# An encoder layer on one core: where softmax's 1/sum and the second sequence's 1/rms are multiplied in

## The chip, the cores and the metric

The kernel runs on one core of a Trainium2 chip. The metric is the device time of one execution in microseconds (us). The core has five engines that run their own instruction queues in order and wait for one another by semaphores: TensorE (PE in the profile; its weight loads are PEld), VectorE (DVE), ScalarE (ACT), GpSimd (POOL) and SyncE (SP), which here issues most of the DMAs. Matmul results land in PSUM, which has eight banks of 128 x 512 fp32 values; everything else is in SBUF or, for data that doesn't fit, in DRAM.

## The reference

One encoder layer is applied to two sequences of 512 tokens (`x_prompt`, sequence 0, and `x_sample`, sequence 1; 1024 channels each) with the same weights, all in fp32:

```python
x = x + 0.5 * swiglu(rms_norm(x, ffn1_norm), ...)
h = rms_norm(x, mix_norm)
proj = h @ w_in            # attention q, k, v; mLSTM q, k, v, gates; output gate; two merge gates
...
s = einsum('bqkgd,bskd->bkgqs', q, k) * scale     # 8 heads of 64, 2 k/v heads
p = softmax(s, axis=-1)
att = einsum('bkgqs,bskd->bqkgd', p, v)
mem = mlstm_bidirectional(...)                    # 4 heads of 128, sigmoid(o_pre) gate
merged = sigmoid(g_att) * (att @ w_up_att) + sigmoid(g_mlstm) * (mem @ w_up_mlstm)
x = x + merged @ w_out
x = x + 0.5 * swiglu(rms_norm(x, ffn2_norm), ...)
```

Two places of it matter here. Softmax divides the exponentials of each row by their sum; the division can as well be done after the product with v. And `rms_norm` multiplies each token's row by 1/rms, a number per token; since `h @ w_in` is linear, that factor can be applied to the row before the projection or to the projection's result.

## The kernel before

**Precision.** PE multiplies in a fast fp32 form that keeps fewer bits, so every operand is kept as a pair, high half and low half: `split` writes high = src rounded by an ACT copy, low = src - high by a DVE subtraction. A product is three matmuls (high x high, high x low, low x high). Channels (or heads) lie on the 128 partitions and the 512 tokens along the columns, except in the token-major projections for k, v and q, where tokens lie on the partitions.

**Order of the stages.** The first FFN serves both sequences together, then `mix(0)` and `mix(1)` do attention, mLSTM, merge and output projection of one sequence each, partly interleaved, and then the second FFN. `mix` is a generator; its callers step it. In the profiled execution the attention of sequence 0 lies at 714 to 824 us, that of sequence 1 at 1106 to 1210 us.

**What decides who runs when.** The program is written as a list of instructions with a priority that follows the program's order; `shifted(n)` gives the instructions inside it a later (or earlier) place by n. A scheduler makes each engine's queue from priorities, dependences, its own costs and free buffers. Buffers come from tagged rings: `t2` has 11 row buffers of 128 x 512, `f2` has 4, the small tiles have a ring each. PSUM has rings too: `MM` 3 banks, `PO` 1, `PS` 2, `PT` 2.

**Units and fill.** A projection by 128 columns of `w_in` is a unit: load (or fetch from DRAM, if sequence 0 has split and parked it) a weight, 24 matmuls into an `MM` bank, and a `done` function that empties the bank. `queue` holds the units for the merge gate of attention (`att_gate`) and the output gate (`out_gate`); `fill(n)` emits n of them between the heads of attention, so that PE has them to work on beside attention's own short chains.

**Where 1/rms is applied.** The rows that enter the projections are x * gain (`emit_hl`, L143), without 1/rms. `r[s]` is 1/rms with tokens on partitions, `R[s]` the same repeated over all partitions with tokens along the columns. Every `done` function multiplies: by `r[s]` as the scale of an ACT copy where tokens lie on partitions (`kv_done`, `q_done`, `mem_values`), by `R[s]` in a DVE multiplication where they lie along the columns (`mem_qk` L918, `out_gate` L927, `att_gate` L1045, `mem_gate` L1091). For sequence 1, `prep1` (L1335) makes the rows' two halves while sequence 0's `merge_mem` runs (after each of its 8 steps): it reads 128 channels of x back from `xbuf` by DMA and calls `emit_hl`.

**Attention.** For each head h, `scores(h)` does for each of four blocks of 128 queries: two matmuls into a `PS` bank (L1001), the negated row maximum on DVE (L1004), the exponential on ACT with the row sum as a second output (L1006), the reciprocal of the sum (L1007) and the scaling of the 128 x 512 exponentials by it in place (L1008), both on DVE. `attend(h)` turns the exponentials, four 128 x 128 transposes into a `PT` bank (L1020) for each of four blocks of keys, splits each bank (L657, L658) and accumulates with v in the one `PO` bank (L1028). The two halves of that bank are added (L1036, L1037) into 64 partitions of `af`; when the odd head of a pair is done, `af` (128 x 512, both heads) is split into `att`. The scores of head h + 1 are emitted ahead of `attend(h)`.

Of the kernel before, what the change touches and what calls it, by code (L numbers as in the profile page):

```python
# [8 lines left out]
F32 = mybir.dt.float32  # L9
F32R = mybir.dt.float32r  # L10
I32 = mybir.dt.int32
AF = mybir.ActivationFunctionType
# [4 lines left out]
P = 128  # L17
# [9 lines left out]
def encoder(ctx, tc, I, outs):  # L27
# [14 lines left out]
    def nm(s):  # L42
        n_id[0] += 1
        return f"{s}_{n_id[0]}"
# [15 lines left out]
    def T2(dtype=F32, tag="t2"):  # L60
        if tag in ("eb", "ac"):
            i = boxes[tag]
            boxes[tag] += 1
            return boxes["tile"][:, i % 4 + (4 if tag == "ac" else 0), :]
        if tag == "R":
            return spool.tile([P, S], dtype, tag="R", bufs=2, name=nm("R"))
        n = {"t2": 11, "f2": 4}[tag]
        return tpool.tile([P, S], dtype, tag=tag, bufs=n, name=nm(tag))
# [50 lines left out]
    def f(ap):  # L119
        return ap.bitcast(F32)  # L120
# [22 lines left out]
    def emit_hl(src, g, k, xh, xl):  # L143
        i1 = nc.scalar.activation(xh[:, k, :], src, AF.Copy, scale=g[:, k:k + 1])
        i2 = nc.vector.scalar_tensor_tensor(xl[:, k, :], src, g[:, k:k + 1], f(xh[:, k, :]),
                                       op0=ALU.mult, op1=ALU.subtract)
        return i1, i2
# [507 lines left out]
    def split(src, hi, lo, eng=None):  # L655

        nc.scalar.activation(hi, src, AF.Copy)  # L657
        (eng or V_).tensor_tensor(lo, src, f(hi), op=ALU.subtract)  # L658
# [4 lines left out]
    NEG = -1e30  # L663

    def small(w, tag):
        return spool.tile([P, w], F32, tag=tag, bufs=2 if tag != "asm" else 6, name=nm(tag))

    gm, g2 = [cpool.tile([P, KD], F32, name=nm("gain")) for _ in range(2)]
    gbias = cpool.tile([P, 16], F32, name="gbias")
# [86 lines left out]
        return p  # L756

    OUT = 3

    def mix(s, xh, xl, early=None, extra=None, after=None):  # L760

# [6 lines left out]

        def F2(dtype=F32):
            return T2(dtype, "f2")  # L770

        def win_cols(c0, done):
            return proj(win_v[:, :, c0:c0 + P], ("in", c0), xsrc, KD, done)
# [38 lines left out]

        def kv_done(pk):
            for b in range(4):
                nc.scalar.activation(kraw3[:, b, :], pk[b][:, 0:P], AF.Copy, scale=r[s][:, b:b + 1])
                nc.scalar.activation(Gt[:, b * 16:(b + 1) * 16], pk[b][:, 2 * P:2 * P + 16], AF.Copy,
                                     scale=r[s][:, b:b + 1])
                pv = pk[b][:, P:2 * P].rearrange("p (k e) -> p k e", k=HK)
                nc.scalar.activation(Vst[:, b, :, 0:DA], pv, AF.Copy, scale=r[s][:, b:b + 1])
                V_.scalar_tensor_tensor(Vst[:, b, :, DA:2 * DA], pv, r[s][:, b:b + 1], f(Vst[:, b, :, 0:DA]),  # L820
                                        op0=ALU.mult, op1=ALU.subtract)
            ssk = small(8, "ssk")
            sumsq(kraw, ssk)
            ko = rope_apply(kraw, rstd_cols(ssk, 8, DA), tabs[1], None)
            ko3 = ko.rearrange("p (g e) -> p g e", e=DA)
            nc.scalar.activation(kst[:, :, 0, 0, :], ko3, AF.Copy)
            nc.scalar.activation(kst[:, :, 0, 1, :], ko3, AF.Copy)
            V_.tensor_tensor(kst[:, :, 1, 0, :], ko3, f(kst[:, :, 0, 0, :]), op=ALU.subtract)
            V_.tensor_tensor(kst[:, :, 1, 1, :], ko3, f(kst[:, :, 0, 1, :]), op=ALU.subtract)
# [3 lines left out]
        def q_done(pq):  # L833
            ssq = small(32, "ssq")
            for b in range(4):
                t = T2()
                nc.scalar.activation(t, pq[b], AF.Copy, scale=r[s][:, b:b + 1])
                sumsq(t, ssq[:, b * 8:(b + 1) * 8])
                qraw.append(t)
            rq.append(rstd_cols(ssq, 32, DA))  # L840
# [56 lines left out]
        def mem_values():  # L897
            def done(pvv):
                vm = A([P, 2, 4, S], F32R, "Vm")
                for b in range(4):  # L900
                    nc.scalar.activation(vm[:, 0, b, :], pvv[b], AF.Copy, scale=r[s][:, b:b + 1])
                    V_.scalar_tensor_tensor(vm[:, 1, b, :], pvv[b], r[s][:, b:b + 1], f(vm[:, 0, b, :]),
                                            op0=ALU.mult, op1=ALU.subtract)
                Vm.append(vm)
            return tok_proj(xh, xl, [(1792, 512)], 2, done)

# [2 lines left out]
        def mem_qk(h, j):  # L909
            def done(pp):  # L910
                if j == 0 and not s:
                    t = wpool.tile([P, 4, S], F32R, tag="w8", bufs=4, name=nm("qk"))
                    qks[h] = [t[:, i] for i in range(4)]
                elif s:
                    t = wpool.tile([P, 2, S], F32R, tag="wr", bufs=4, name=nm("qk"))
                    qks.setdefault(h, []).extend(t[:, i] for i in range(2))
                t = F2()
                V_.tensor_tensor(t, pp, R[s], op=ALU.mult)  # L918
                split(t, *qks[h][2 * j:2 * j + 2])
            return win_cols((768, 1280)[j] + h * P, done)  # L920

        ogs = {}
# [1 line left out]
        def out_gate(h):  # L924
            def done(pp):
                og = T2(F32, "ac")
                V_.tensor_tensor(og, pp, R[s], op=ALU.mult)  # L927
                nc.scalar.activation(og, og, AF.Tanh, scale=0.5)
                G_.tensor_scalar(og, og, 1.0, hn[:, h:h + 1], op0=ALU.add, op1=ALU.mult)
                ogs[h] = og  # L930
            return win_cols(2320 + h * P, done)
# [60 lines left out]
        att = A([P, 4, 2, S], F32R, "att")  # L992
        afs = {}

        def scores(h):
            hk = h // 4
            Ps = []
            for b in range(4):
                p = PS()
                for j in range(2):  # L1000
                    nc.tensor.matmul(p, qT[:, h, b * P:(b + 1) * P], kv[:, hk * 2 + j, :],  # L1001
                                     start=(j == 0), stop=(j == 1))
                c = small(3, "asm")
                V_.tensor_reduce(c[:, 0:1], p, axis=AX.X, op=ALU.max, negate=True)  # L1004
                e = T2()
                nc.scalar.activation(e, p, AF.Exp, bias=c[:, 0:1], accum_out=c[:, 1:2])  # L1006
                V_.reciprocal(c[:, 2:3], c[:, 1:2])  # L1007
                V_.tensor_scalar(e, e, c[:, 2:3], None, op0=ALU.mult)  # L1008
                Ps.append(e)
            return Ps  # L1010

        def attend(h, Ps):
            hk = h // 4
            po = PO()
            turned = []
            for kb in range(4 + 1):
                if kb < 4:
                    p = PT()
                    for b in range(4):
                        nc.tensor.transpose(p[:, b * P:(b + 1) * P], Ps[b][:, kb * P:(kb + 1) * P], ident)  # L1020
                    ph, pl = T2(F32R), T2(F32R)
                    split(p, ph, pl)
                    turned.append((kb, ph, pl))
                if kb >= 1:
                    kv_, *pp = turned.pop(0)
                    with shifted(50):
                        for i, w in enumerate(pp):
                            nc.tensor.matmul(po, Vst[:, kv_, hk, :], w, start=(kv_ == 0 and i == 0),  # L1028
                                             stop=(kv_ == 3 and i == 1))
            if h % 2 == 0:  # L1030
                afs[0] = T2(F32, "f2")
            af = afs[0]
            o0 = (h % 2) * DA
            o1 = DA - o0
            t = T2(F32, "f2")
            nc.scalar.activation(t[o0:o0 + DA, :], po[o1:o1 + DA, :], AF.Copy)  # L1036
            V_.tensor_tensor(af[o0:o0 + DA, :], po[o0:o0 + DA, :], t[o0:o0 + DA, :], op=ALU.add)  # L1037
            if h % 2:
                split(af, att[:, h // 2, 0, :], att[:, h // 2, 1, :])

        mg = A([P, KD, S], F32, "mg")

        def att_gate(d):
            def done(pp):
                V_.tensor_tensor(mg[:, d, :], pp, R[s], op=ALU.mult)  # L1045
                nc.scalar.activation(mg[:, d, :], mg[:, d, :], AF.Tanh, scale=0.5)
            return win_cols(2832 + d * P, done)

        queue.extend(att_gate(d) for d in range(KD))
# [38 lines left out]
        def mem_gate(d):  # L1088
            def done(pp):
                t = ths[d] = T2()  # L1090
                V_.tensor_tensor(t, pp, R[s], op=ALU.mult)  # L1091
                nc.scalar.activation(t, t, AF.Tanh, scale=0.5)
            return win_cols(3856 + d * P, done)

        def merge_mem(d):
# [239 lines left out]
    def prep1(d):  # L1335
        if d == 0:
            nhl[1] = xhl_tiles()
        xt = T2(F32, "f2")
        nc.sync.dma_start(xt, xbuf[1][:, d, :])
        emit_hl(xt, gm, d, *nhl[1])  # L1340

    ffn_down(I["ffn1_w_down"][0], rbuf[0], up.ring, tail, xbuf, done1, 7, mix_consts)

# [178 lines left out]
```

## Time and profile before

| | us |
|---|---|
| median of 3 runs | 2084.76 |
| lowest, highest | 2084.72, 2087.68 |
| the profiled execution's own time | 2083.45 |
| its span, first to last instruction | 2081.4 |
| PE busy | 2060.3 |
| DVE busy | 1573.6 |
| ACT busy | 895.4 |

The span is what the profile's views divide up; the profiled execution's time is 2.05 us longer than it. In the views a row of a group names line, engine, operation, result and operands, shapes and count, then the busy time of all in us and the mean of one in ns, then how long the engine stood idle before them and what ended that. A row by stage gives a stretch of the span, its length, and for each engine the busy time and the number of instructions in it. In a row of waits the engine and line that waited stand left of the arrow, who ended the wait right of it. Matmuls are pipelined: the recorded length of one reaches into the next, so start times tell their pace.

### The profile page before, as it was taken

The page shows a single profiled execution, that of the slowest core. Times are in us where ns is not written, and L with a number is a line of the kernel's source. Part 1 is how long each engine was busy: PE and PEld are TensorE (multiplying, and loading weights), DVE is VectorE, ACT ScalarE, POOL GpSimd, SP SyncE. Part 2 cuts the span into 40 slices and gives each one's busy share as a digit, 9 for nine tenths or more (in the row PEclk, how much of TensorE's full clock was granted, in tenths as well). Part 3 has the DMA queues.
Part 4 walks back from the last instruction along what each step waited for, and adds up shares of the span by engine and source line. Part 5 has one row for each costly group of instructions (what it writes and reads, how often), then busy time and mean ns, then how long its engine had stood idle before and what let it go on. Part 6 is the DMA issues. An engine that isn't in the chain of part 4 may idle for free.

```text
span 2081.4 us, 27314 instructions
## 1 busy us (share of the span) xinstructions
PE 2060.3 (99%) x9488; PEld 1694.0 (81%) x9488; DVE 1573.6 (76%) x2870; ACT 895.4 (43%) x1645; POOL 111.2 (5%) x122
## 2 busy tenths in 40 slices
PE   8999999999999999999999999999999999999998
PEld 6888888888888877888887788888888888888887
DVE  7888888786797899575568846555788888785797
ACT  6544444443234566463344543324444444442222
POOL 1000000001003012100120000002000000000010
PEclk9999999999999999999999999999999999999999
DMA  8656555699766655777685345677656555599753
GB/s 277 208 171 195 193 171 182 201 346 359 260 223 243 216 167 198 257 240 272 214 283 193 112 153 188 208 258 244 200 177 201 193 172 182 187 339 350 273 189 117
DMA packets 303161, 458.52 MB, mean 220 GB/s; under 512 B 20304, under 2 KB 170848, under 8 KB 302000
## 3 DMA queue, kind: packets, MB, share of 16 engines
q1 hardware_dynamic: 301152, 451.32, 64.4%
q0 software_dynamic: 1872, 5.46, 0.8%
q8 instruction: 75, 1.23, 0.2%
q14 instruction: 62, 0.51, 0.1%
HBM read 289.82 MB, written 166.89 MB: 219 GB/s over the span
## 4 chain that ended last, share of the span: by engine, by line
PE 92%; DVE 3%; DMA 3%; ACT 1%; issue 1%; SPq 0%; POOL 0%; DVEq 0%; ACTq 0%; POOLq 0%
PE mm L755 19%; PE pss L333 17%; PE pst L333 11%; PE mm L333 10%; PE mm L589 9%; PE pst L589 4%; PE pss L589 4%; PE mm L739 4%; PE pso L589 3%; PE pso L739 1%; PE pso L1028 1%; PE pso L1167 1%; PE pst L755 1%; PE pss L755 1%; PE pss L1117 1%; PE pst L1020 1%
## 5 line engine op out<-in xcount | busy, mean ns | idle before, releaser
L755 PE MATMUL mm<-xh,w 128*128 128x512 f32 x896 | 290.6, 394 | 0.0
L333 PE MATMUL pss<-xc,w 128*128 128x512 f32 x1056 | 256.4, 392 | 0.2 <-DVE t L364 0.2
L333 PE MATMUL mm<-xc,w 128*128 128x512 f32 x1056 | 253.5, 391 | 2.2 <-ACT w L291 1.4
L333 PE MATMUL pst<-xc,w 128*128 128x512 f32 x1056 | 253.8, 390 | 0.1
L333 PEld LDWEIGHTS pss<-xc,w 128*128 128x128 f32 x1056 | 197.0, 188 | 47.4 <-DVE t L364 6.7
L333 PEld LDWEIGHTS mm<-xc,w 128*128 128x128 f32 x1056 | 197.4, 188 | 45.2 <-ACT w L291 2.3
L333 PEld LDWEIGHTS pst<-xc,w 128*128 128x128 f32 x1056 | 198.2, 188 | 41.6 <-ACT t L368 0.5
L755 PEld LDWEIGHTS mm<-xh,w 128*128 128x128 f32 x896 | 167.4, 188 | 33.6
L589 PE MATMUL mm<-rt,w 128*128 128x512 f32 (+1 forms) x819 | 188.4, 385 | 0.0
L755 PE MATMUL mm<-xl,w 128*128 128x512 f32 x448 | 176.0, 393 | 0.0
L589 PEld LDWEIGHTS mm<-rt,w 128*128 128x128 f32 x819 | 151.4, 188 | 29.8
L291 ACT ACTIVATE w<-t 128x512 fp32r<-128x512 f32 x176 | 106.9, 627 | 138.6 <-issue 55.2
L292 DVE TENSOR_TENSOR w<-t,w 128x512 fp32r<-128x512 f32 x176 | 118.3, 689 | 55.1 <-ACT w L291 53.1
L333 PE MATMUL pss<-xc,f 128*128 128x512 f32 x528 | 126.9, 389 | 0.0
L333 PEld LDWEIGHTS pss<-xc,f 128*128 128x128 f32 x528 | 99.1, 188 | 20.6
L657 ACT ACTIVATE w<-wr 128x512 fp32r<-128x512 f32 x72 | 45.1, 632 | 138.6 <-PE pso L589 70.8
L657 ACT ACTIVATE w<-t 128x512 fp32r<-128x512 f32 x82 | 51.8, 632 | 107.6 <-PE pst L589 62.4
L755 PEld LDWEIGHTS mm<-xl,w 128*128 128x128 f32 x448 | 84.3, 188 | 16.7
L589 PE MATMUL pst<-rt,w 128*128 128x512 f32 x396 | 93.7, 389 | 0.0
L589 PE MATMUL pss<-rt,w 128*128 128x512 f32 x396 | 93.7, 389 | 0.0
L589 PEld LDWEIGHTS pst<-rt,w 128*128 128x128 f32 x396 | 74.3, 188 | 15.4
L589 PEld LDWEIGHTS pss<-rt,w 128*128 128x128 f32 x396 | 74.3, 188 | 15.4
(337 smaller groups left out, 3666.9 us busy)
## 6 DMA issues: line engine op xcount, KB each, us to landing
rt<-rbuf SPq DMA_DIRECT2D x154, 512.0 KB, 5.5
wpark<-w SPq DMA_DIRECT2D x104, 512.0 KB, 3.6
w<-wpark SPq DMA_DIRECT2D x104, 512.0 KB, 4.8
wr<-in_ffn_w_gate_dram SPq DMA_DIRECT2D x62, 512.0 KB, 5.3
rbuf<-tab SPq DMA_DIRECT2D x102, 256.0 KB, 3.8
wr<-in_ffn_w_up_dram SPq DMA_DIRECT2D x44, 512.0 KB, 4.7
rbuf<-f SPq DMA_DIRECT2D x72, 256.0 KB, 3.7
wr<-in_w_in_dram SPq DMA_DIRECT2D x36, 512.0 KB, 5.7
```

What stands on the lines that cost most here:

```text
L291: pin(nc.scalar.activation(t[:, 0], src, AF.Copy))
L292: pin(V_.tensor_tensor(t[:, 1], src, f(t[:, 0]), op=ALU.subtract))
L333: nc.tensor.matmul(p, a[:, k, :], xt[:, b, k, :], start=(first and k == 0 and i == 0), stop=(k == HK_ - 1 and i == 2), skip_group_check=True)
L589: nc.tensor.matmul(p, u[:, a, d * P:(d + 1) * P], r[:, b, ts], start=(first and q == 0 and k == 0), stop=(q == len(us) - 1 and k == 2), sk ...
L657: nc.scalar.activation(hi, src, AF.Copy)
L739: nc.tensor.matmul(p[b][:, :N], a[:, k, bs], w_[:, kl, :], start=(k == 0 and i == 0), stop=(k == KD - 1 and i == 2))
L755: nc.tensor.matmul(p, a[:, k, :], b, start=(k == 0 and i == 0), stop=(k == n - 1 and i == 2))
L1020: nc.tensor.transpose(p[:, b * P:(b + 1) * P], Ps[b][:, kb * P:(kb + 1) * P], ident)
L1028: nc.tensor.matmul(po, Vst[:, kv_, hk, :], w, start=(kv_ == 0 and i == 0), stop=(kv_ == 3 and i == 1))
L1117: nc.tensor.matmul(p, qk[a][:, isl], qk[b], start=(n == 0), stop=(n == 2))
L1167: nc.tensor.matmul(po, vm[:, a, t, hs_], b, start=(t == 0 and n == 0), stop=(t == 3 and n == 2))
```

## The change

Softmax's division is moved. The exponentials go into the transposes as they are. The row sums of a pair of heads are collected in one small tile `asum` (128 queries x 4 blocks x 2 heads). When the odd head of the pair has been added into `af`, DVE takes the reciprocal of the 8 columns, ACT writes them out repeated 64 times each into a 128 x 512 buffer (`wide`), PE turns that with four transposes into a `PT` bank (so that each of the pair's 128 partitions has its head's 1/sum along the tokens), DVE multiplies `af` by the bank, and `af` is split as before. All that follows the reciprocal is shifted by 30 places in priority. The ring of the maxima gets 4 buffers of one column instead of 6 of three.

For sequence 1 alone (`NORMED = (1,)`), the rows are multiplied by gain and 1/rms in one DVE instruction (`normed`, which the kernel has for the second FFN) and then split, ACT copy and DVE subtraction, where before ACT scaled the high half by the gain and DVE made the low half in one scalar_tensor_tensor. After the projections of sequence 1 nothing is multiplied by 1/rms any more: the ACT copies have scale 1, the q/k units of the mLSTM split straight from the PSUM bank, and the tanh of the gates reads the bank. Sequence 0 keeps its multiplications.

```diff
-        return spool.tile([P, w], F32, tag=tag, bufs=2 if tag != "asm" else 6, name=nm(tag))
+        return spool.tile([P, w], F32, tag=tag, bufs=2 if tag != "asm" else 4, name=nm(tag))
...
+    NORMED = (1,)
...
+        def col_scale(b):
+            return 1.0 if s in NORMED else r[s][:, b:b + 1]
+
+        def split_cols(src, b, hi, lo):
+            if s in NORMED:
+                return split(src, hi, lo)
+            nc.scalar.activation(hi, src, AF.Copy, scale=r[s][:, b:b + 1])
+            V_.scalar_tensor_tensor(lo, src, r[s][:, b:b + 1], f(hi), op0=ALU.mult, op1=ALU.subtract)
+
+        def scaled_row(pp, to):
+            if s in NORMED:
+                return pp
+            t = to()
+            V_.tensor_tensor(t, pp, R[s], op=ALU.mult)
+            return t
...
             def done(pp):       # mem_qk
-                t = F2()
-                V_.tensor_tensor(t, pp, R[s], op=ALU.mult)
-                split(t, *qks[h][2 * j:2 * j + 2])
+                split(scaled_row(pp, F2), *qks[h][2 * j:2 * j + 2])
...
             def done(pp):       # att_gate; out_gate and mem_gate likewise
-                V_.tensor_tensor(mg[:, d, :], pp, R[s], op=ALU.mult)
-                nc.scalar.activation(mg[:, d, :], mg[:, d, :], AF.Tanh, scale=0.5)
+                nc.scalar.activation(mg[:, d, :], scaled_row(pp, lambda: mg[:, d, :]), AF.Tanh, scale=0.5)
...
         def scores(h):
             hk = h // 4
             Ps = []
+            if h % 2 == 0:
+                asums[h // 2] = small(8, "asum").rearrange("p (b u) -> p b u", u=2)
...
-                c = small(3, "asm")
-                V_.tensor_reduce(c[:, 0:1], p, axis=AX.X, op=ALU.max, negate=True)
+                c = small(1, "asm")
+                V_.tensor_reduce(c, p, axis=AX.X, op=ALU.max, negate=True)
                 e = T2()
-                nc.scalar.activation(e, p, AF.Exp, bias=c[:, 0:1], accum_out=c[:, 1:2])
-                V_.reciprocal(c[:, 2:3], c[:, 1:2])
-                V_.tensor_scalar(e, e, c[:, 2:3], None, op0=ALU.mult)
+                nc.scalar.activation(e, p, AF.Exp, bias=c, accum_out=asums[h // 2][:, b, h % 2:h % 2 + 1])
...
             if h % 2:           # attend
-                split(af, att[:, h // 2, 0, :], att[:, h // 2, 1, :])
+                inv = asums[h // 2]
+                V_.reciprocal(inv, inv)
+                with shifted(30):
+                    wide = T2(F32, "f2")
+                    nc.scalar.activation(wide.rearrange("p (b u e) -> p b u e", u=2, e=DA),
+                                         inv.unsqueeze(3).to_broadcast([P, 4, 2, DA]), AF.Copy)
+                    pr = PT()
+                    for b in range(4):
+                        nc.tensor.transpose(pr[:, b * P:(b + 1) * P], wide[:, b * P:(b + 1) * P], ident)
+                    V_.tensor_tensor(af, af, pr, op=ALU.mult)
+                    split(af, att[:, h // 2, 0, :], att[:, h // 2, 1, :])
...
             nhl[1] = xhl_tiles()       # prep1
         xt = T2(F32, "f2")
         nc.sync.dma_start(xt, xbuf[1][:, d, :])
-        emit_hl(xt, gm, d, *nhl[1])
+        normed(xt, gm, R[1], d)
+        split(xt, nhl[1][0][:, d, :], nhl[1][1][:, d, :])
```

More of the change, by code (lines that the diff above doesn't have):

```diff
@@ L814, in kv_done @@
             for b in range(4):
-                nc.scalar.activation(kraw3[:, b, :], pk[b][:, 0:P], AF.Copy, scale=r[s][:, b:b + 1])
-                nc.scalar.activation(Gt[:, b * 16:(b + 1) * 16], pk[b][:, 2 * P:2 * P + 16], AF.Copy,
-                                     scale=r[s][:, b:b + 1])
+                rsc = col_scale(b)
+                nc.scalar.activation(kraw3[:, b, :], pk[b][:, 0:P], AF.Copy, scale=rsc)
+                nc.scalar.activation(Gt[:, b * 16:(b + 1) * 16], pk[b][:, 2 * P:2 * P + 16], AF.Copy, scale=rsc)
                 pv = pk[b][:, P:2 * P].rearrange("p (k e) -> p k e", k=HK)
-                nc.scalar.activation(Vst[:, b, :, 0:DA], pv, AF.Copy, scale=r[s][:, b:b + 1])
-                V_.scalar_tensor_tensor(Vst[:, b, :, DA:2 * DA], pv, r[s][:, b:b + 1], f(Vst[:, b, :, 0:DA]),
-                                        op0=ALU.mult, op1=ALU.subtract)
+                split_cols(pv, b, Vst[:, b, :, 0:DA], Vst[:, b, :, DA:2 * DA])
             ssk = small(8, "ssk")
@@ L836, in q_done @@
                 t = T2()
-                nc.scalar.activation(t, pq[b], AF.Copy, scale=r[s][:, b:b + 1])
+                nc.scalar.activation(t, pq[b], AF.Copy, scale=col_scale(b))
                 sumsq(t, ssq[:, b * 8:(b + 1) * 8])
@@ L900, in done @@
                 for b in range(4):
-                    nc.scalar.activation(vm[:, 0, b, :], pvv[b], AF.Copy, scale=r[s][:, b:b + 1])
-                    V_.scalar_tensor_tensor(vm[:, 1, b, :], pvv[b], r[s][:, b:b + 1], f(vm[:, 0, b, :]),
-                                            op0=ALU.mult, op1=ALU.subtract)
+                    split_cols(pvv[b], b, vm[:, 0, b, :], vm[:, 1, b, :])
                 Vm.append(vm)
@@ L926, in done @@
                 og = T2(F32, "ac")
-                V_.tensor_tensor(og, pp, R[s], op=ALU.mult)
-                nc.scalar.activation(og, og, AF.Tanh, scale=0.5)
+                nc.scalar.activation(og, scaled_row(pp, lambda: og), AF.Tanh, scale=0.5)
                 G_.tensor_scalar(og, og, 1.0, hn[:, h:h + 1], op0=ALU.add, op1=ALU.mult)
@@ L993, in mix @@
         afs = {}
+        asums = {}
         def scores(h):
@@ L1090, in done @@
                 t = ths[d] = T2()
-                V_.tensor_tensor(t, pp, R[s], op=ALU.mult)
-                nc.scalar.activation(t, t, AF.Tanh, scale=0.5)
+                nc.scalar.activation(t, scaled_row(pp, lambda: t), AF.Tanh, scale=0.5)
             return win_cols(3856 + d * P, done)
```

## The prediction

> **What bounds the kernel now.** I read the page first (busy time, granted clock, chain), then a table by stage, then single TensorE starts.
>
> ```profile
> span 2081.4 us, 27314 instructions
> PE 2060.3 (99%) x9488; PEld 1694.0 (81%) x9488; DVE 1573.6 (76%) x2870; ACT 895.4 (43%) x1645; POOL 111.2 (5%) x122
> PEclk9999999999999999999999999999999999999999
> PE 92%; DVE 3%; DMA 3%; ACT 1%; issue 1%; SPq 0%; POOL 0%; DVEq 0%; ACTq 0%; POOLq 0%
> ```
>
> TensorE (PE) is busy for 99% of the span at full clock and makes up 92% of the chain that ended last. So the question for every edit is whether it changes PE's work or PE's waits; VectorE (DVE) time counts only where PE waits for it. But a busy PE is not a PE at its pace: a matmul that starts late is hidden in the modelled end of the one before. So I take the pace from start times (timeline of PE; start, length, then the instructions merged into the row):
>
> ```profile
> 980.16 2.88 PE L755 MATMUL pss<-mem,w 128*128 128x512 f32 x12
> 982.88 0.39 PE L755 MATMUL pst<-mem,w 128*128 128x512 f32 x1
> ...
> 703.26 1.03 PE L941 MATMUL pst<-ident,t 128*128 128x128 f32 x8
> 704.05 0.47 PE L755 MATMUL mm<-xh,w 128*128 128x512 f32 x1
> ```
>
> Twelve matmuls of 512 columns take 982.88 - 980.16 = 2.72 us, 0.227 each; eight transposes take 704.05 - 703.26 = 0.79 us, 0.099 each. Now the stages that the change touches. In the table by stage 714 to 824 is the attention of sequence 0, 980 to 1006 the merge with the preparation of sequence 1's rows, 1106 to 1210 the attention of sequence 1; the second pair of rows is the same view for the transpose bank `pst` alone.
>
> ```profile
> core 0: us, PE busy (x) PEld busy (x) DVE busy (x) ACT busy (x) POOL busy (x), PEclk, DMA share, GB/s
> 714.00:824.00 110.00, 107.83 (x537) 85.31 (x536) 103.03 (x215) 68.45 (x141) 16.82 (x11) 1.00 0.58 186
> 980.00:1006.00 26.00, 26.00 (x131) 22.23 (x130) 21.72 (x28) 11.77 (x18) 9.47 (x6) 1.00 0.50 168
> 1106.00:1210.00 104.00, 103.32 (x514) 82.85 (x513) 87.49 (x202) 56.34 (x127) 0.69 (x1) 1.00 0.39 130
> 1210.00:1366.00 156.00, 156.00 (x733) 127.75 (x732) 77.19 (x223) 54.83 (x132) 2.08 (x3) 1.00 0.58 186
> ...
> 714.00:824.00 110.00, 23.09 (x152) 18.18 (x152) 22.94 (x34) 20.78 (x36) 1.00 0.58 186
> 1106.00:1210.00 104.00, 20.41 (x136) 16.41 (x136) 23.35 (x34) 18.61 (x32) 1.00 0.39 130
> ```
>
> Attention 0 holds 152 transposes and 537 - 152 = 385 long matmuls: 152 x 0.099 + 385 x 0.227 = 102.4 us of pace in 110, so 7.6 us are lost. Attention 1: 136 x 0.099 + 378 x 0.227 = 99.3 in 104, 4.7 us lost. Together 12.3 us. DVE is at 103.03 of 110 us (94%) and 87.49 of 104 (84%) there: the second bound, close behind PE. In the two other stages shown it is at 84 and 49%. Who PE waited for in the two attentions (view of waits, first attention 0, then attention 1: waiter, releaser, us in total, times, longest):
>
> ```profile
> PE pst L1020 <- DVE t L658: 1.1, 1, 1.1
> PEld pso L1028 <- ACT t L657: 2.8, 5, 0.9
> PEld pst L1020 <- DVE t L658: 1.8, 5, 0.5
> PEld pss L1001 <- ACT t L1006: 1.6, 6, 0.5
> PEld pso L1028 <- DVE t L658: 0.5, 2, 0.3
> ACT t L1006 <- DVE asm L1004: 8.9, 10, 2.6
> ...
> PEld pss L1001 <- ACT t L1006: 1.9, 3, 1.1
> PEld pso L1028 <- DVE t L658: 1.0, 4, 0.3
> PEld pst L1020 <- DVE t L658: 0.8, 3, 0.3
> ```
>
> The transposes wait for DVE to empty a transpose bank (L658 frees it), the scores wait for the exponential (L1006), and that one waits for DVE's maximum (L1004, 8.9 us). What a freer DVE can reach: 1.1 + 1.8 + 1.6 + 0.5 = 5.0 us in attention 0 and 1.9 + 1.0 + 0.8 = 3.7 in attention 1, 8.7 together.
>
> **The change, part by part.** Costs per instruction (view of groups: count, busy us, mean ns):
>
> ```profile
> L1008 DVE TENSOR_SCALAR t<-t,asm 128x512 f32<-128x512 f32 x64 | 33.2, 522 | 0.4
> L1007 DVE RECIPROCAL asm<-asm 128x1 f32<-128x1 f32 x64 | 9.7, 156 | 1.4 <-ACT t L1006 1.1
> L1020 PE MATMUL pst<-ident,t 128*128 128x128 f32 x256 | 39.3, 274 | 1.3 <-DVE t L658 1.1
> L1176 DVE TENSOR_TENSOR box<-box,pst 128x512 f32<-128x512 f32 x8 | 5.5, 683 | 2.9 <-PE pst L213 2.9
> L657 ACT ACTIVATE att<-f 128x512 fp32r<-128x512 f32 x8 | 5.0, 624 | 2.3 <-DVE f L1037 2.3
> L1045 DVE TENSOR_TENSOR mg<-mm,R 128x512 f32<-128x512 f32 x16 | 10.9, 684 | 1.0 <-PE mm L755 0.9
> L1091 DVE TENSOR_TENSOR t<-mm,R 128x512 f32<-128x512 f32 x16 | 11.1, 691 | 46.6 <-PE mm L755 46.5
> L918 DVE TENSOR_TENSOR f<-mm,R 128x512 f32<-128x512 f32 x16 | 11.0, 687 | 21.9 <-PE mm L755 21.9
> L927 DVE TENSOR_TENSOR box<-mm,R 128x512 f32<-128x512 f32 x8 | 5.5, 690 | 5.5 <-PE mm L755 5.4
> L145 DVE SCALAR_TENSOR_TENSOR xl<-f,gain,xh 128x512 fp32r<-128x512 f32 x8 | 7.0, 884 | 0.0
> L653 DVE SCALAR_TENSOR_TENSOR f<-f,gain,R 128x512 f32<-128x512 f32 x8 | 5.8, 741 | 0.0
> ```
>
> *Softmax, DVE.* Removed: 64 scalings and 64 reciprocals, 33.2 + 9.7 = 42.9 us, half in each attention. Added for the 8 pairs of heads: 8 small reciprocals (8 x 0.156 = 1.2) and 8 multiplications with a PSUM operand (as L1176, 5.5). Net -36.2, 18.1 per attention: DVE falls to about 85 of 110 and 69 of 104 us, less the gate multiplications below. The scaling also stood between exponential and transpose, so each block is ready 0.68 us sooner. That is worth only the waits that it ends: bounds 0 (another wait stands behind each) and the 8.7 us above. I take half, 4.3, because in the same rows L1028 also waits 2.8 us for ScalarE's (ACT's) copy L657, whose work is not lessened.
>
> *Softmax, PE.* Added: 4 transposes x 4 pairs x 2 sequences = 32, which nothing covers on a PE that is never short of work: 32 x 0.099 = +3.2 us. Their durations (L1020) would say 32 x 0.274 = 8.8; but the next matmul starts long before a transpose's modelled end, so I take the pace.
> The Trainium skill, page "TensorE: Matmul & The Clock Gate", section "Part 4: PE-mode transpose", says that a transpose took about 275 ns in one kernel and that full clock does not engage for transposes. By that the 32 would cost 8.8 us rather than 3.2. The trace agrees on the duration and not on the pace.
>
> *Softmax, the new chain.* Per pair: reciprocal (DVE), widening copy (ACT, about L657's 0.62 us, 5.0 us in all, on an engine that is at 54 to 62% there), 4 transposes (PE), multiplication (DVE), split (ACT, DVE, as before but after it). What PE can lose by it is the third use of a pair of transpose banks: from 0 (in the timeline above the eight transposes follow the matmul before them without a gap) to 1.1 us a pair (the longest wait for such a bank). Nearer to 0, since DVE has gained 18 us of room: I take 0.15, 8 x 0.15 = +1.2 us. Behind the multiplication in DVE's queue stand the next head's maxima and splits; if its transposes are late, they wait too, and that is what the 1.1 bounds. The result `att` is first read by the up-projection after attention, so its shift costs nothing until the last pair; there the gate matmuls of the queue (fill) cover it. The smaller ring for the maxima (4 instead of 6) costs nothing: a maximum now dies with its exponential, one head has 4 of them. The pair's output and the widened sums occupy the 4 "f2" buffers longer; in sequence 1 the q/k units no longer use these.
>
> *Sequence 1 normalised before the split.* Removed: 28 multiplications (8 of L1045, 8 of L1091, 8 of L918, 4 of L927), 28 x 0.69 = 19.3 us of DVE, spread over stages where PE loses nothing to them (the rows 1210 to 1366: PE 156.00 of 156, DVE 77.19). So 0, at most a part of the 8.7 already counted. The q/k split now reads its bank twice (copy 0.62, subtraction 0.69 instead of one 0.69); a unit of 24 matmuls lasts 24 x 0.227 = 5.4 us and there are three such banks: 0. The tanh reads PSUM directly: shorter.
> Added, in sequence 0's merge: 8 multiplications of 0.741 = 5.9 us of DVE, while the subtraction gets cheaper (0.884 to about 0.69, -1.6). No DMA is added: the 8 reads of `xbuf` stay. DVE there goes from 21.72 to 26.0 of 26 us. What covers it:
>
> ```profile
> 996.32 1.40 DVE L145 SCALAR_TENSOR_TENSOR xl<-f,gain,xh 128x512 fp32r<-128x512 f32 x1
> 1001.92 0.41 PE L739 MATMUL mm<-w,xh 128*128 128x272 f32 x2
> ```
>
> The last low half is ready at 997.7, and sequence 1's first projection starts at 1001.92 and works through the eight row blocks in order, 24 matmuls each; the last block is needed last. 4.3 us later is still in time. If that cover were gone it would cost up to 4.3 us.
>
> **The sum.** +3.2 (transposes) + 1.2 (banks) - 4.3 (waits) + 0 (second part) = +0.1 us on a span of 2081.4. The profiled execution took 2083.45 us, so 2083.55. The median of the runs before is 2084.76, 1.3 above the profiled execution; on that scale the forecast is 2084.9.
>
> **Rivals.**
> 1. *All of the waits go.* For it: DVE at 94% in attention 0, and both PE waits lead back to DVE. Against it: ACT's copies and PE's own order. 3.2 + 0 - 8.7 = -5.5: 2079.3. The floor, all 12.3 us gone, is 2075.7.
> 2. *The bank wait takes their place (the other side).* Place: `pr` holds one of the two transpose banks through a DVE queue, eight times. Price: 8 x 1.1 = 8.8, so 3.2 + 8.8 - 4.3 = +7.7: 2092.5 (2096.8 without the gain). It decides "slower" from (4.2 + 4.3 - 3.2) / 8 = 0.66 us a pair. For it: this very wait is the longest of PE in attention 0. Against it: DVE was at 94% then.
> 3. *DVE is late at the seam (980 to 1006).* It fills up to 26 of 26 us: 0.1 + 4.3 = +4.4: 2089.2. Against it: the late rows are needed last.
> 4. *The 32 transposes cost their full duration.* As the four starts in the first timeline contradict it, little is left: 0.1 + 8.8 - 3.2 = +5.7: 2090.5. This is the result that the Trainium skill's transpose figure (page and section above) would give.
> 5. *The second part does nothing to the time*: it is already in the forecast at 0.
>
> **How the numbers follow.** A measurement of this kernel tells about 0.2% (4.2 us) from no change. Forecast 0.62 (within), rival 1 0.15 (faster), rival 2 0.15, rival 3 0.05, rival 4 0.03 (slower, 0.23). The forecast's own range, regain from 8.7 x 0.2 to 8.7 x 0.8 and banks from 0.35 to 0 a pair, is 2081 to 2089. The range that holds 8 in 10 goes from rival 1's value to rival 2's: 2079 to 2092.5.
>
> **What would show it.** In the changed profile: 32 more matmuls on PE; the two attention stages with DVE near 85 us and, without the 8 gate multiplications too, 64 us; L1020's and L1001's waits for DVE and for the exponential at about half; no PE wait for the transpose bank over 0.5 us at the new transposes; PE without a gap around the seam and no change in the stages after attention. The forecast is wrong if PE's order changes with DVE's load so that gate matmuls no longer stand where the attention waits, or if the new multiplication waits for PE with the next head's maxima behind it.

## The result, and the profile after

The changed kernel takes 2094.24 us in the median (2093.22 to 2096.11) beside 2084.94 for the kernel before in the same comparison: +9.3 us, a ratio of 1.0042 with a 95% interval of 1.0031 to 1.0054. It is slower, by 0.4%, and the forecast (2084.9, range 2079.0 to 2092.5) was wrong; the range misses the time by 1.7 us. The profiled execution took 2094.29 us, 10.8 more than that of before.

The page of the changed kernel (span; busy time, share and instructions of each engine; shares of the chain that ended last):

```profile
span 2091.7 us, 27288 instructions
PE 2066.9 (99%) x9520; PEld 1696.4 (81%) x9520; DVE 1538.5 (74%) x2738; ACT 895.4 (43%) x1653; POOL 105.7 (5%) x122
PE 93%; DMA 2%; DVE 2%; ACT 1%; issue 0%; SPq 0%; POOL 0%; DVEq 0%; POOLq 0%; ACTq 0%
```

The 32 matmuls more are there (9520 against 9488), DVE has lost 35 us and 132 instructions, PE is still at 99% and is still the chain. PE's busy time is up by 6.6 us, but where the other loss lies the page doesn't say; that shows only in the table by stage. Same columns as in the prediction: the stretch, its length, busy time (instructions) of PE, PEld, DVE, ACT, POOL, then PEclk, DMA share, GB/s. Changed kernel, attention 0, the seam, the start of attention 1 in three pieces, and the stage after it:

```profile
714.00:824.00 110.00, 108.92 (x546) 85.67 (x546) 87.99 (x157) 69.28 (x143) 15.02 (x11) 1.00 0.58 186
980.00:1006.00 26.00, 26.00 (x127) 22.02 (x126) 22.11 (x28) 10.23 (x17) 8.10 (x6) 1.00 0.59 196
1106.00:1114.20 8.20, 3.96 (x18) 2.95 (x16) 6.34 (x11) 1.35 (x4) 0.00 (x0) 1.00 0.83 256
1114.20:1118.40 4.20, 4.12 (x13) 3.23 (x14) 3.42 (x6) 2.25 (x7) 0.00 (x0) 0.61 0.61 195
1118.40:1122.00 3.60, 3.60 (x19) 2.92 (x18) 2.79 (x5) 1.45 (x4) 0.00 (x0) 0.98 0.32 73
1218.00:1374.00 156.00, 156.00 (x734) 127.76 (x733) 69.97 (x213) 56.20 (x139) 2.54 (x3) 1.00 0.57 181
```

For PE, attention 0, the seam and the stage after attention look much as before. The third row doesn't: in 8.2 us PE is busy for 3.96. In the fourth PE is "busy" again, but the granted clock is 0.61: it has 13 matmuls and transposes in 4.2 us, where the row below, at clock 0.98, has 19 in 3.6 us.

I measure the stages by starts from here on: each attention from its first score matmul to its last output matmul. Of the four new transposes of the last pair none lies in this stretch, so it holds 12 of the 16 new ones. Attention 0 went from 108.8 to 109.5 us, attention 1 from 103.5 to 111.5, the three stretches between and behind by +0.4, +1.0 and +0.6, the two FFNs together by -0.4. So 8.0 of the 10.3 us of span are in attention 1. The view of waits for 1090 to 1120 (waiter, releaser, us in total, times, longest), changed kernel and then the kernel before:

```profile
DVE box L977 <- DMA box<-ebuf: 7.1, 4, 3.9
ACT t L1020 <- DVE asm L1018: 7.1, 3, 6.0
PE pss L1015 <- ACT t L1020: 4.3, 1, 4.3
```

```profile
ACT t L1006 <- DVE asm L1004: 3.8, 5, 1.5
DVE box L967 <- DMA box<-ebuf: 1.5, 1, 1.5
PE pss L1001 <- ACT t L1006: 0.7, 1, 0.7
```

Read from the bottom up: PE waits 4.3 us for the exponential (L1020) to give a score bank free, the exponential 6.0 us for DVE's maximum (L1018), and DVE four times for a DMA. That DMA (`mem_rows`) brings a row of `ebuf` for the memory stage: mask addition (L977, on DVE for sequence 1), then two row maxima (L982, L983). None of it is wanted by attention; it is work for the next stage that stands in the same queue. The timeline of DVE (start, length, instructions; in brackets the idle time before it and what ended that), changed kernel:

```profile
1102.04 0.69 DVE L977 TENSOR_TENSOR box<-box,tab 128x512 f32<-128x512 f32 x1 [3.94 <-DMA box<-ebuf]
...
1105.83 0.69 DVE L977 TENSOR_TENSOR box<-box,tab 128x512 f32<-128x512 f32 x1 [1.31 <-DMA box<-ebuf]
...
1108.06 0.69 DVE L977 TENSOR_TENSOR box<-box,tab 128x512 f32<-128x512 f32 x1 [0.35 <-DMA box<-ebuf]
...
1111.46 0.69 DVE L977 TENSOR_TENSOR box<-box,tab 128x512 f32<-128x512 f32 x1 [1.52 <-DMA box<-ebuf]
1112.07 0.69 DVE L658 TENSOR_TENSOR qk<-mm,qk 128x512 fp32r<-128x512 f32 x1
1112.67 1.28 DVE L1018 TENSOR_REDUCE asm<-pss 128x1 f32<-128x512 f32 x2
```

The kernel before, the same view:

```profile
1101.48 0.69 DVE L967 TENSOR_TENSOR box<-box,tab 128x512 f32<-128x512 f32 x1 [1.53 <-DMA box<-ebuf]
...
1103.88 0.68 DVE L967 TENSOR_TENSOR box<-box,tab 128x512 f32<-128x512 f32 x1
...
1105.66 0.68 DVE L918 TENSOR_TENSOR f<-mm,R 128x512 f32<-128x512 f32 x1
1106.26 1.28 DVE L1004 TENSOR_REDUCE asm<-pss 128x1 f32<-128x512 f32 x2
...
1108.13 0.67 DVE L967 TENSOR_TENSOR box<-box,tab 128x512 f32<-128x512 f32 x1
```

Before, two rows stand ahead of the first score maximum, and the third comes after two of them. In the changed kernel three whole rows and the mask addition of a fourth stand ahead of it, and the fourth has to wait until 1111.46 for its data. Its DMA was issued only at 1107.15: SyncE waits for a row buffer until DVE has read an earlier row out of it (L983, here at 1106.44). Of DVE's four waits only the last two, 0.35 and 1.52 us, fall behind the first score matmul; the rest of the maximum's delay is the rows' own work on DVE. The first maximum moves from 1106.26 to 1112.67, while the first score matmul moves only from 1104.5 to 1106.6. What PE does meanwhile, and behind the wait (changed kernel, timeline of PE):

```profile
1109.35 0.61 PE L755 MATMUL mm<-xh,w 128*128 128x512 f32 x2
1114.28 0.73 PE L1015 MATMUL pss<-kv,qT 128*128 128x512 f32 x2 [4.32 <-ACT t L1020]
1114.85 0.38 PE L1032 MATMUL pst<-ident,t 128*128 128x128 f32 x2
1114.98 1.06 PE L1015 MATMUL pss<-kv,qT 128*128 128x512 f32 x2
1115.84 0.63 PE L1032 MATMUL pst<-ident,t 128*128 128x128 f32 x2
1116.12 0.78 PE L755 MATMUL mm<-xl,w 128*128 128x512 f32 x1
1116.70 1.05 PE L755 MATMUL mm<-xh,w 128*128 128x512 f32 x2
1117.55 0.63 PE L755 MATMUL mm<-xl,w 128*128 128x512 f32 x1
1117.98 0.63 PE L755 MATMUL mm<-xh,w 128*128 128x512 f32 x1
1118.40 0.70 PE L1015 MATMUL pss<-kv,qT 128*128 128x512 f32 x2
```

The rows from 1114.28 to 1118.40 hold 9 long matmuls and 4 transposes, at full pace 9 x 0.227 + 4 x 0.099 = 2.4 us; they take 4.1. At 1116.70 two matmuls start 0.425 us apart, not 0.227. So the wait costs 4.3 us of idleness and 1.7 us more at the lower clock behind it, 6.0 together, where the wait of before cost 0.7.

### The profile page after: what moved, and what is told of

The parts are those of the page before. It is cut to its first block, busy times and chain, and to the rows that moved or that the text cites. A ratio compares the mean times of both kernels' runs of the same rounds, so it can differ in the third digit from the quotient of the medians.

```text
span 2091.7 us, 27288 instructions
## 1 busy us (share of the span) xinstructions
PE 2066.9 (99%) x9520; PEld 1696.4 (81%) x9520; DVE 1538.5 (74%) x2738; ACT 895.4 (43%) x1653; POOL 105.7 (5%) x122
## 4 chain that ended last, share of the span: by engine, by line
PE 93%; DMA 2%; DVE 2%; ACT 1%; issue 0%; SPq 0%; POOL 0%; DVEq 0%; POOLq 0%; ACTq 0%
PE mm L755 19%; PE pss L333 17%; PE pst L333 11%; PE mm L333 10%; PE mm L589 9%; PE pst L589 4%; PE pss L589 4%; PE mm L739 4%; PE pso L589 3%; PE pso L739 1%; PE pso L1040 1%; DMA box<-ebuf 1%; PE pss L1015 1%; PE pso L1187 1%; PE pst L1032 1%; PE pst L755 1%
## 5 line engine op out<-in xcount | busy, mean ns | idle before, releaser
L239 ACT ACTIVATE w<-wr 128x1024 fp32r<-128x1024 f32 (+1 forms) x56 | 57.4, 1028 | 75.0 <-PE mm L755 30.7
```

What stands on the lines that cost most here:

```text
L239: pin(nc.scalar.activation(hi, raw, AF.Copy))
```

## The experiments

Theory A: the loss is the order of DVE's queue at the start of attention 1 (rows of the memory stage ahead of score maxima, each waiting for its DMA), plus 32 transposes at PE's pace. Theory B, the prediction's second and fourth rivals: the transposes cost more than their pace, by the wait for their bank or by their full duration, in every pair. Theory C, used for the last three runs: the two parts together harm each other in some way that is not the rows.

**One part alone.** e1 is the change without its second part, e2 without its first:

```diff
 e1:
-    NORMED = (1,)
+    NORMED = ()
...
-        normed(xt, gm, R[1], d)
-        split(xt, nhl[1][0][:, d, :], nhl[1][1][:, d, :])
+        emit_hl(xt, gm, d, *nhl[1])
 e2: scores() and the end of attend() as before
+                V_.reciprocal(c[:, 2:3], c[:, 1:2])
+                V_.tensor_scalar(e, e, c[:, 2:3], None, op0=ALU.mult)
...
-                    V_.tensor_tensor(af, af, pr, op=ALU.mult)
```

> Only the softmax part of the change; sequence 1 keeps its multiplications by 1/rms. Theory A (the time comes from the 32 transposes and from one long wait at the start of attention 1, which the second part causes): +3 to +4 us on before, about 2088.5, and no PE idle stretch over 1 us at the start of attention 1. Theory B (the bank that the new chain holds is what costs): nearly all of the loss, +8 to +10 us, about 2094.

> Only the second part; softmax scales its exponentials as before. Theory A: +5 to +6 us on before, about 2090.5, with PE idle for about 4 us ahead of the third score block of attention 1 and some 4 us at a lower granted clock behind it. Theory B: within 1 us of before.

e1: 2090.25 us (before, run beside it: 2085.24), ratio 1.0024 [1.0015, 1.0033], +5.0. e2: 2090.34, 1.0024 [1.0015, 1.0033], +5.1. Together that is 10.1, beside +9.3 for the whole. Waits at the start of attention 1, e1 and then e2 with a row by stage behind the wait:

```profile
PE pss L1015 <- ACT t L1020: 2.0, 1, 2.0
DVE box L977 <- DMA box<-ebuf: 2.9, 1, 2.9
```

```profile
PE pss L1013 <- ACT t L1018: 3.4, 1, 3.4
DVE box L977 <- DMA box<-ebuf: 6.2, 4, 2.3
1112.40:1116.40 4.00, 3.94 (x12) 3.16 (x13) 3.83 (x11) 2.13 (x7) 0.00 (x0) 0.63 0.58 222
```

The second part alone, which adds no work to PE, brings the four waits of DVE for rows, PE's wait and the low clock. Without it (e1) DVE waits for one row only, but longer than before (2.9 us against 1.5), and PE waits 2.0 instead of 0.7. Theory A had expected no wait over 1 us in e1, so there it missed; the wait explains 1.3 of the +5.0, the transposes (below) 3.5.

**The new chain taken out, and its transposes four times.** e4 leaves out the division by the sums altogether (reciprocal, widening, transposes, multiplication); e5 turns each block four times, 96 transposes more than the change.

```diff
 e4:
-                inv = asums[h // 2]
...
-                    V_.tensor_tensor(af, af, pr, op=ALU.mult)
-                    split(af, att[:, h // 2, 0, :], att[:, h // 2, 1, :])
+                split(af, att[:, h // 2, 0, :], att[:, h // 2, 1, :])
 e5:
-                    for b in range(4):
+                    for b in (0, 1, 2, 3) * 4:
```

> The change without the new chain: no reciprocal, no widened sums, no 32 transposes, no multiplication of the pair's output, so the attention output is not divided by its row sums. Theory A: 3.2 to 4.4 us less than the change, about 2090, with the long wait still there. Theory B: 8 to 10 us less, back at about 2085.

> The change, with each of the 32 new transposes issued four times into the same bank, so 96 more on TensorE. At the pace of the trace of before (0.099 us) +9.5 us on the change, about 2103.7; at their recorded duration (0.274 us) +26 us, about 2120; 0 if the new transposes stand in idle time.

e5: 2104.33 us (before, run beside it: 2085.88), ratio 1.0086 [1.0072, 1.0100], +18.4, which is 9.1 more than the change's +9.3: 9.1 / 96 = 0.095 us for a transpose. That is a little low, since PE waits only 2.9 us at the start of attention 1 here instead of 4.3; with these 1.5 us added it is 0.110. In the profiled runs attention 0 is 5.06 us longer than in the changed kernel with 36 transposes more in it, 0.141 each, of which 0.8 us in all are longer waits of PE (0.118 without them); attention 1 is 2.48 us longer, and would be 3.94 longer with an equal wait, 0.109 each. The timeline of PE has 16 of them between 744.28 and 746.00, 0.108 each:

```profile
744.28 1.97 PE L1059 MATMUL pst<-ident,f 128*128 128x128 f32 x16
746.00 1.17 PE L1015 MATMUL pss<-kv,qT 128*128 128x512 f32 x4
```

So 32 cost 3.0 to 3.8 us (3.5 below), and the duration in the records (0.27) is not their price. e4: 2092.51, ratio 1.0033 [1.0021, 1.0046], +7.3, only 2.0 less than the change, although it has no more work on PE than the kernel before, and less on DVE than either. It still waits 2.9 us at the start of attention 1, and its attention 0 lasts 111.3 us (before: 108.8): there PE waits up to 1.6 us for a transpose bank. With 15 us less of DVE work in it attention 0 came out longer. A new layout of the queues would explain that, but no run shows it. Less DVE work, by itself, bought nothing. Theory B falls: e5 rules out the full duration, and e4 brought 2.0 us where the wait for the bank would have brought 8 to 10. Theory A's 3.2 to 4.4 was too high too.

**The rows held back.** If the order of DVE's queue is the cause, moving the rows must remove the loss and leave the arithmetic alone. In e3 the DMA of head 0's rows in sequence 1 can't start before the scores of head 0 exist: GpSimd copies one column of the exponentials into the row's buffer first, so that the scheduler has to place the rows later. e6, e7 and e8 are the kernel before, the second part alone and the softmax part alone with the same edit.

```diff
-        def mem_rows(h, d):
+        def mem_rows(h, d, behind=None):
             eb = T2(F32, "eb")
+            if behind is not None:
+                G_.tensor_copy(eb[:, 0:1], behind)
...
-            eb3, em3 = mem_rows(h, d)
+            eb3, em3 = mem_rows(h, d, first[0] if s and h == 0 else None)
...
         Ps = scores(0)
+        first = [Ps[3][:, 0:1]]
```

> The change, but the loads of the mLSTM's gate rows for mem_max in sequence 1 are held back until the exponentials of head 0 are there (a GpSimd copy of one column into the buffer ahead of its DMA), so that their mask additions stand behind the maxima in DVE's queue. Theory A: the long wait goes, -5 to -6 us on the change, about 2088.5. Theory B: no change, about 2094.

> The kernel before, with the gate rows of sequence 1's mem_max held back until the exponentials of head 0 are there. Theory A: the wait at the start of attention 1 was already 0.8 us in the kernel before, so -0.5 to -1 us, about 2084.5; the theory that holding the rows only moves the wait: 0 or slower.

> The second part alone (sequence 1 normalised before the split), with the rows held as in the run before. Theory A: nearly all of its +5.1 us was the wait at the start of attention 1, so 0 to +1.5 us on before, about 2086. If the seam (VectorE full while sequence 1's rows are made) or the later stages cost: still +4 to +5.

> The softmax part alone, with the rows held. Theory A: the transposes and their handover remain, +3 to +4 us on before, about 2088.5, as its own +5.0 held 1.3 us more of the same wait than before. If the waits did go down with VectorE's load: +1 or less.

e6: 2084.76 (before, run beside these: 2085.88), ratio 0.9995 [0.9986, 1.0003]: on the kernel before the edit does nothing measurable. e7: 2085.12, 0.9996 [0.9987, 1.0005]: the second part's +5.1 is gone, to within the interval of about 2 us either way. So it was, in the main, the wait at the start of attention 1: e2's 3.4 us and some 1.5 at the lower clock, less the 0.7 of before, are 4.2 of it. e8: 2088.34, 1.0011 [1.0002, 1.0019], +2.5: about the price of the transposes, and 2.5 less than e1. e3, both parts: 2090.10, 1.0020 [1.0011, 1.0028], +4.9, better than the change by 4 us, but not by what e7 and e8 would add up to (+1.7). Waits of PE in attention 1 in e3, and of DVE for rows:

```profile
PE pss L1017 <- ACT t L1022: 1.1, 1, 1.1
PE pst L213 <- DVE rs L192: 0.5, 1, 0.5
PE pso L1042 <- DVE t L658: 0.2, 1, 0.2
DVE box L979 <- DMA box<-ebuf: 1.5, 1, 1.5
```

The rows have moved into the attention, and DVE still waits there for one, with PE behind it. Theory A had expected 2088.5.

**The rows elsewhere.** e9 spreads them (those of head k behind the attention of pair k - 1), e10 is the second part alone with the same, e11 holds only the first ones, until the scores of head 1. `mem_rows` is as in e3.

```diff
 e9, e10:
+            eb3, em3 = mem_rows(h, d, None if not s else first[0] if h == 0 else f(att[:, h - 1, 0, 0:1]))
 e11: as e3, and in the loop over the heads
+            if h == 0:
+                first[0] = nxt[3][:, 0:1]
```

> The changed kernel, with the gate rows of every head of sequence 1 held: the first head's until the first scores exist, those of head k until the pair k - 1 of the attention is read. VectorE's queue then has at most one or two rows between two heads' maxima. Theory A (each mask addition waits for its row in front of score maxima, and TensorE pays the longest of these waits; the 32 transposes remain): the 1.1 us wait that the run with only the first rows held kept is gone too, and the time comes to 32 x 0.105 = 3.4 us over the kernel before, less the 0.8 by which the held rows came out under it in the run with the norm alone: +2.5, 2088.4. Theory C (the two parts together hurt each other by something other than the rows): it stays where the first held version was, +4.9, 2090.8.

> The second part alone (the old softmax), with the rows held and spread in the same way. Theory A: no TensorE work is added and the wait at the start of attention 1 is away, so as the run with the first rows held: 0 to -1 us against before, 2084 to 2085; if the spread rows give more, it is from the 5.6 us that attention 1 still loses against its pace, at most 3 us: 2082. Theory C: also about 2085, it says nothing else here.

> The changed kernel, with the first gate rows of sequence 1 held longer than in the first held version, until the scores of head 1 exist; the later ones are not held. Theory A: the rows' waits only move behind the maxima of head 1 and stand there in a block as in the first held version: +3 to +5 us, 2089 to 2091, with one TensorE wait of about 1 us a little later than before. Theory C: +4.9, 2090.8, without such a wait.

e9: 2093.18 (before, run beside these: 2085.53), 1.0038 [1.0025, 1.0051], +7.6, against +2.5 expected of theory A. e10: 2084.81, 0.9999 [0.9991, 1.0008], as expected. e11: 2087.38, 1.0008 [0.9999, 1.0017], +1.9, better than either theory had it. Both misses come from the same thing, when a row's data arrives, in opposite directions. PE's waits in attention 1 and one row of DVE's timeline in e9:

```profile
PE pss L1017 <- ACT t L1022: 2.8, 2, 1.6
PE pst L1034 <- DVE t L658: 1.6, 1, 1.6
...
1141.68 0.69 DVE L979 TENSOR_TENSOR box<-box,tab 128x512 f32<-128x512 f32 x1 [3.40 <-DMA box<-ebuf]
```

Held to the end of a pair, a row is placed right behind its own DMA: DVE waits 3.4 us for it at 1141.68 and PE stands still for 1.65. I had counted how many rows stand between two heads, and not when their data comes. In e11 the row by stage for all of attention 1 is:

```profile
1108.00:1214.00 106.00, 105.78 (x525) 83.49 (x525) 71.80 (x138) 56.71 (x127) 0.98 (x3) 1.00 0.42 137
```

PE is busy for 105.78 of 106.00 us at clock 1.00, and the view of waits names none for PE. That gives the test of theory A over all the kernels with both parts (length of attention 1 by starts; PE's waits by the timeline and the view of waits):

| kernel | attention 1, us | over e11 | PE's waits there, us |
|---|---|---|---|
| e11 | 105.31 | 0 | 0 |
| e3 | 107.24 | 1.93 | 1.15 + 0.51 + 0.24 = 1.90 |
| e9 | 109.95 | 4.64 | 1.20 + 1.65 + 1.64 = 4.49 |
| changed | 111.49 | 6.18 | 4.32 + 1.68 at low clock = 6.00 |

All four have the same 148 transposes and 374 long matmuls in this stretch, and the waits account for the differences to 0.2 us. (By medians, each over the kernel before beside it, e3, e9 and the change lie 3.0, 5.7 and 7.4 us above e11, some 1.1 to 1.2 more than attention 1 shows; the intervals are that wide.) Theory A holds as to the place and the price, theory C isn't needed. None of these versions beats the kernel before: the best with the second part (e7, e10) can't be told from it.

## Why the prediction was wrong

*Bound, and transposes.* That PE bounds the kernel was right, and so was +3.2 for the transposes: measured 3.5. By the Trainium skill's figure (page "TensorE: Matmul & The Clock Gate", section "Part 4: PE-mode transpose") the estimate would have been 8.8; the trace agrees with its 275 ns as a duration (273 ns in the median of L1059) and not as a price, and rival 4 falls.

*Handover of the transpose bank.* Taken at +1.2 (0.15 a pair), with 0.66 a pair as the point where rival 2 decides. Waits of the weight loads in attention 0 of the changed kernel:

```profile
PEld pso L1040 <- ACT t L657: 2.1, 6, 0.6
PEld pss L1015 <- ACT t L1020: 2.0, 8, 0.6
PEld pst L1032 <- DVE t L658: 1.2, 5, 0.4
PEld pst L1059 <- ACT f L1055: 1.1, 3, 0.6
```

The new transposes wait at most 0.6 us, for ACT's widening copy and not for the bank. The bank that they fill makes later transposes' weight loads wait for DVE's multiplication (L1060), three times in both attentions, 1.1 us in all, not 1.1 a pair. Rival 2's time (2092.5) was near the result by coincidence; its mechanism was not what happened.

*DVE's relief.* The prediction's rows add up to 36.2 + 19.3 - 4.3 = 51.2 us less for DVE; the page shows 35.1 less, and attention 0 15.0 (103.03 to 87.99) where 18.1 was forecast. DVE's records reach into one another as PE's do: L918 at 1105.66 is recorded with 0.68 us, and the next instruction starts 0.60 us later. The prediction priced PE by starts and DVE by recorded lengths.

*The waits regained, -4.3.* This term was mis-sized: it is between 0 and 1. The same rows show why: the wait for DVE at the transposes fell from 1.8 to 1.2 us and L1040's for ACT's copy from 2.8 to 2.1, but the scores' wait for the exponential rose from 1.6 to 2.0, and L1059's is new. Attention 0 is 0.7 us longer with 12 more transposes in it (12 x 0.108 = 1.3), so 0.6 at most was regained there. That is too little to read from single traces: e10, e2, e7 and e6, with the same work for PE as the kernel before, take 108.8 to 110.2 us for it. In attention 1 without any wait (e11) it is +1.8 with 12 transposes more and one long matmul fewer (1.1): nothing regained. By medians e8 costs 2.5 where its transposes alone are worth 3.5. e4, with DVE relieved and no chain at all, regained nothing either. Even e11, in which PE waits for nobody by the view, takes 105.3 us where its pace is 148 x 0.099 + 374 x 0.227 = 99.6; so most of what the prediction counted as lost against the pace is not such waits, and no run says what it is. Rival 1 falls.

*The second part, 0.* This is the step that failed. "Spread over stages where PE loses nothing to them" was true of the time that DVE saved, and I stopped there. Some of the removed multiplications stood in DVE's queue around the start of attention 1 (L918's at 1105.66 in the row above, right ahead of the first maximum). Without them the queue was laid out with three rows and a half of the memory stage ahead of the first score maximum, each waiting for a DMA. Price: +5.1 alone (e2), and gone when the rows are held back (e7). Rival 5 ("does nothing to the time") falls with it. I had named a changed order of PE as what would make the forecast wrong; it was the order of DVE that changed, with PE paying.

*The seam.* Right in effect: PE is busy for 26.00 of 26.00 us. DVE came to 22.11 there, not to 26: only four of the eight new multiplications lie in the stretch, the others ran earlier, from 920.7 on. Rival 3 falls.

*The sum.* 3.5 (transposes), 6.0 - 0.7 = 5.3 (the wait and the low clock), together 8.8 of +9.3. The forecast of +0.1 missed by 9.2: the wait that it had at 0 (5.3) and the regain that did not come (4.3), less the 1.2 that it had allowed for the banks, are 8.4 of it. The remaining 0.5 is not placed for certain. A candidate is the stretch from sequence 1's first projection to its first score matmul: 102.6 us before and in e1, 103.6 in the changed kernel, 102.9 to 103.4 in the other kernels with the second part (e2, e7, e10, e11). PE's waits there are 0.9 us in the changed kernel and 0.3 before, all for DVE. Open too is why e1's row lands later than before, and which rule of the scheduler turns the missing multiplications into the other order; the runs show that the order is the cause of the loss, not how it came about.

## What to carry to other kernels

An instruction that is taken out of a queue which a scheduler lays out doesn't only save its time: look at what stands behind it, and whether something that waits for a DMA can slide ahead of what the bound engine is waiting for. Such work for a later stage should be held back until its data has surely come; placed right behind its own DMA (e9) it only carries the wait along. Price added matmuls by the distance of starts, DVE's instructions too, and a wait of some 3 us on a busy PE at more than its length (here 1.7 us more).

## What the runs showed of the hardware

The clock drops after a wait in the middle of the kernel, with 99% of the span busy. After waits of 2.9 us (e4, e5), 3.4 (e2) and 4.3 (changed kernel) the clock stood at one half for a while; after e1's 2.0 us and e9's waits of 1.2 to 1.65 us it stayed at 1.00. Rows by stage behind the wait, e1, then e4, then the changed kernel:

```profile
1111.90:1116.00 4.10, 4.07 (x22) 3.20 (x22) 3.95 (x7) 2.10 (x6) 0.00 (x0) 1.00 0.77 261
```

```profile
1117.00:1119.00 2.00, 2.00 (x7) 1.66 (x6) 1.71 (x3) 1.30 (x4) 0.00 (x0) 0.50 0.51 170
```

```profile
1114.28:1115.10 0.82, 0.82 (x5) 0.69 (x6) 0.82 (x3) 0.61 (x2) 0.00 (x0) 1.00 0.85 327
1115.10:1118.50 3.40, 3.40 (x12) 2.63 (x11) 2.52 (x5) 1.56 (x4) 0.00 (x0) 0.51 0.53 158
```

So in the changed kernel PE went on at full clock for 0.8 us after the wait and then had half the clock for 3.4 us, which cost 1.7. In e4 it is 3.4 us at 0.50 as well (1115.90 to 1119.30). The Trainium skill, page "TensorE: Matmul & The Clock Gate", section "Part 1: The HAM clock gate", says that an idle window of about 3.4 us halves the clock and a busy one of about that length restores it, and that the windows run on freely. The trace agrees on the half and on the 3.4 us until full clock is back. On the idle time it differs: by the view of waits, which begins at the modelled end of the matmul before, 2.9 us was already enough, and 2.0 was not.
